# A hybrid decoder trunk: the 16x16 inverses on GpSimd, and an output projection cut at 12 of its 16 row tiles

## The chip, the cores and the metric

One core of a Trainium2 chip. The metric is the device time of one execution in microseconds (us), as a median of several. The matrix engine is TensorE (PE in the rows; PEld is its weight load), the vector engine VectorE (DVE), the scalar engine ScalarE (ACT), the general engine GpSimd (POOL); SyncE (SP) issues the weight loads from HBM.

## What is computed

Two decoder layers over 256 tokens of width 2048. Layer 0's mixer, the one that the change touches, has two halves behind one input projection: 8 HGRN2 heads (a gated linear recurrence) and 8 gated DeltaNet heads. Cut to what matters:

```
def gated_delta_chunked(q, k, v, beta, g):           # the "gdn" heads
    a_mat = einsum(kb, k) * decay * strict           # strictly lower triangular
    t_mat = triangular_solve(eye + a_mat, eye)       # the inverse of a unit triangle
    w, u  = t_mat @ (kb * exp(gam)), t_mat @ (v * beta)
    ...                                              # recurrence over chunks

def hgrn2_gdn_mixer(u, ...):
    proj = u @ w_in                                  # 2048 x 8208
    o_a = gated_head_norm(hgrn2_chunked(...))        # 8 heads, 1024 columns
    o_b = gated_head_norm(gated_delta_chunked(...))  # 8 heads, 1024 columns
    return concatenate([o_a, o_b]) @ w_out           # 2048 x 2048

def reference(x, ...):
    for layer in range(2):
        h = h + mixer(rmsnorm(h))                    # hgrn2 + gdn, then mamba2
        h = h + memory_cross_attention(rmsnorm(h))
        h = h + swiglu(rmsnorm(h))
    return rmsnorm(h)
```

All is float32.

## The kernel before

**Projections.** Every weight streams once from HBM in tiles of 128 partitions x 1024 numbers (two row tiles of 512 columns), named `wr`. `split` makes two reduced-precision parts of each: ScalarE casts it (`wh`), VectorE subtracts (`wl <- wr, wh`, both read from SBUF). Four buffers each of wr, wh and wl let this run a few tiles ahead. `xstat` then does six products for each row tile into two accumulators in PSUM (`acc`): these are called projection products below, and 12 of them use up one tile of wl. `project` calls `xstat` for four blocks of 512 output columns (`nb`), and VectorE adds each accumulator to the residual `h`; behind a block, a `done` function may turn it for the next layer's norm.

**The first mixer** (`hybrid`) runs `gdn(0)`, `gdn(1)`, `hgrn(0)`, `hgrn(1)`, each a group of four heads, and then the output projection, in two calls of `project`: row tiles 8 to 15 (the two gdn groups, `yb`), then 0 to 7 (the two hgrn groups, `ya`), the second with `done`. A group's small work (decays, masks, norms) is a chain over all engines. While a chain runs, TensorE does projection products of whatever is independent of it.

**The inverse in `gdn(g)`.** Four heads' triangular matrices `M` go to DRAM and come back as 64 diagonal blocks of 16x16, one to a partition (`U`). Starting from the identity in `x`, 15 steps of a multiplication into `w` and a subtraction from `x` invert them all; each needs the one before it. A copy turns the result over. The two go to DRAM (`scratch`, two stores) and return as `X` and `XT`, two DMAs each, all issued by GpSimd. Then three levels of products on TensorE (`mx <- XT, b` is each level's first) put together the whole inverse. `tt(pool, B, M, mb)` on GpSimd makes `b` (`b <- MD,big` in the rows).

**`hgrn(g)`** goes through seven levels; in each VectorE makes `tmp <- cv`, ScalarE takes the exponential, GpSimd multiplies the halves with k and q (`tmp <- tmp,kq`), and TensorE makes products. q comes over `tn` transposes and ScalarE's copy `kq <- tn`. The group ends in `finish`: products with `S` (`mx <- vt,D` or `uf,D`), `head_norm` (squares on ScalarE, sums and a reciprocal root in small steps on VectorE, scaled rows `b <- mx,hms,gate`, transposes `mx <- cst,b` on TensorE) and `head_out`.

**What sets the order.** The program is written in the order above; a list scheduler, working from modelled durations, then fixes for each engine the order in which its instructions stand. On the chip every engine takes its own in that order and waits at an instruction whose input isn't there. TensorE's place for a chain's next product is thus a count of projection products ahead of it. Names such as `b` stand for small scratch buffers of a pool.

Of the kernel before, what the change touches and what calls it, by code (L numbers as in the profile page):

```python
# [14 lines left out]
ALU = mybir.AluOpType  # L15
# [4 lines left out]
D = 2048  # L20
T = 256
KT = D // P
# [6 lines left out]
for _name, _w in (("norm_mix", 32), ("norm_xattn", 32), ("norm_mem", 32), ("norm_ffn", 32), ("norm_final", 16),  # L29
# [12 lines left out]

BLOCKS = {
    "hy_w_in": [(0, KT, n, 512) for n in range(0, 8192, 512)] + [(0, KT, 8080, P)],
    "hy_w_out": [(k, 8, n, 512) for k in (0, 8) for n in range(0, D, 512)],
    "ssd_w_in": ([(0, KT, n, 512) for n in range(0, 8192, 512)] + [(0, KT, n, 512) for n in range(8192, 10240, 512)]
                 + [(0, KT, 10176, P)]),
    "ssd_w_out": [(k, KT, n, 512) for k in (0, KT) for n in range(0, D, 512)],
# [9 lines left out]
FIRST = {}  # L58
# [20 lines left out]
def trunk(ctx: ExitStack, tc: tile.TileContext, A: dict, out: bass.AP):  # L79
    nc = tc.nc  # L80
    pe, act, dve, pool = nc.tensor, nc.scalar, nc.vector, nc.gpsimd
# [42 lines left out]
    def tt(e, o, a, b, op):  # L124
        e.tensor_tensor(o, a, b, op=op)  # L125
# [54 lines left out]
            mm(acc, wl, xh, False, k == KT - 1)  # L180
        return acc

    def xstat(W, n0, n, u, k0=0, nk=KT):

        accs = [pa.tile([P, n], F32, name="acc", tag="acc") for _ in range(2)]
        for k, wh, wl in wtiles(W, k0, nk, n0, n):
            for a in range(2):
                xh = u[k // 4][0][:, k % 4, a * P:(a + 1) * P]
                xl = u[k // 4][1][:, k % 4, a * P:(a + 1) * P]
                mm(accs[a], xh, wh, k == 0, False)  # L190
                mm(accs[a], xh, wl, False, False)
                mm(accs[a], xl, wh, False, k == nk - 1)
        return accs
# [125 lines left out]
    def blk(W, nb):  # L319
        return W[nb * 512:(nb + 1) * 512, :].rearrange("(k p) t -> p k t", p=P)  # L320

    def project(W, u, k0, nk, done=None, parts=None):
        for nb in range(4):
            n = 256 if nb == 3 and (W[0], k0, nb * 512, 512) not in FIRST else 512
            for c in range(0, 512, n):
                for a, acc in enumerate(xstat(W, nb * 512 + c, n, u, k0, nk)):
                    hb = h[nb][:, a, c:c + n]
                    tt(dve, hb, hb, acc, ALU.add)
                    if parts:
                        parts(nb, a, c, n)  # L330
            if done:
                done(nb)
# [130 lines left out]
    def hybrid(N, nxt):  # L463
# [47 lines left out]
        def gdn(g):  # L511
# [60 lines left out]
            for k in range(15):  # L572
                n, r = 15 - k, k + 1
                o, e = x[:, 0, 0:r, r:16], w[:, 0:r, r:16]
                tt(dve, e, x[:, 0, 0:r, k:r].to_broadcast([64, r, n]),
                   U[:, k:r, r:16].to_broadcast([64, r, n]), ALU.mult)
                tt(dve, o, o, e, ALU.subtract)
            dve.tensor_copy(x[:, 1].rearrange("p a b -> p b a"), x[:, 0])
            X = t4("X", [P, 2, 4, P])
            XT = t4("XT", [P, 2, 4, P])  # L580
            for q, (d, t) in enumerate(((d_x, X), (d_t, XT))):
# [135 lines left out]
        tt(dve, lb[:, 0], e2[:, 0], mx, ALU.mult)  # L717
        dve.tensor_scalar(lb[:, 1], lb[:, 0], -1.0, 1.0, op0=ALU.mult, op1=ALU.add)

        ya = [hgrn(0), hgrn(1)]  # L720
        Wo = ("hy_w_out", 0)
        project(Wo, yb, 8, 8)
        project(Wo, ya, 0, 8, lambda nb: nxt.block(nb, h[nb]))


    mem_r = []

    def xattn(layer, N, nxt):
# [43 lines left out]
        for i in range(2):  # L772
# [3 lines left out]
                for b in range(2):  # L776
                    mm(ps[:, x], v[:, b, m * P:(m + 1) * P], pT[b][:, m], x == 0 and b == 0, b == 1)
            split(hi[:, 2 * i:2 * i + 2], lo[:, 2 * i:2 * i + 2], ps)
        project(("xa_wo", layer), [(hi, lo)], 0, 4, lambda nb: nxt.block(nb, h[nb]))


    def ffn(layer, N, done=None, parts=None):
        b0 = 0
        for nblk in (4, 4, 3):
# [21 lines left out]
                late = sg  # L806
            turn(late)
            last = b0 + nblk == 11
            project(("ffn_w_down", layer), hid, 4 * b0, 4 * nblk, done if last else None, parts if last else None)
            b0 += nblk  # L810


    def ssd(N, nxt):
# [89 lines left out]
            ys.append(group(g, bct))  # L903
        r = ssa.column(2 * D)
        for nb in range(4):
            accs = xstat(Wo, nb * 512, 512, ys, KT)
            for a in range(2):
                p, hb = part[nb][:, a], h[nb][:, a]
                tt(dve, p, p, accs[a], ALU.add)
                stt(hb, p, r[:, a:a + 1], hb, ALU.mult, ALU.add)  # L910
            nxt.block(nb, h[nb])
# [115 lines left out]
```

## Time and profile before

| | |
|---|---|
| median of 3 runs | 2978.18 us (2977.99 to 2978.61) |
| the profiled execution | 2979.66 us, of which the span is 2977.9 us |
| first mixer (to the last transposes of its output) | 0 to about 595 us |
| TensorE | busy 2943.9 us, 99% of the span |
| VectorE, ScalarE, GpSimd | 58%, 51%, 9% |
| granted TensorE clock over the span | 0.996 |

The span runs from the first to the last instruction; the profiled execution's own time is 1.8 us above it. Times in rows count from the start of the span. Busy time of TensorE includes overlap of neighbouring products, so what it lacks to the span is only part of what it loses.

### The profile page before, as it was taken

How to read it: one execution, taken by the hardware profiler on the slowest of the kernel's cores; microseconds unless marked ns; L12 is line 12 of the kernel's file. 1: busy time of each engine (PE TensorE's matmuls, PEld its weight loads, DVE VectorE, ACT ScalarE, POOL GpSimd, SP SyncE). 2: the span in 40 equal slices, each digit the busy share in tenths (PEclk: the TensorE clock that was granted, in tenths of full speed). 3: DMA queues.
4: the chain of work that ended last, by engine and by line, in shares of the span. 5: the costliest groups of instructions: out<-in, count | busy, mean ns of one | idle time of the engine just before them, and what ended most of it. 6: DMA issues, size and time to landing. Idle time of an engine off the chain costs nothing.

```text
span 2977.9 us, 36564 instructions
## 1 busy us (share of the span) xinstructions
PE 2943.9 (99%) x13948; PEld 2443.6 (82%) x13948; DVE 1736.4 (58%) x2138; ACT 1517.2 (51%) x1939; POOL 258.8 (9%) x211
## 2 busy tenths in 40 slices
PE   9999999999999999999999999999999999999998
PEld 7888788788888888888888788878888888888887
DVE  6665568766455445455666646666665454455455
ACT  7545545565443443344567645766555444443444
POOL 1011203210000000000022300231000000000000
PEclk9999999999999999999999999999999999999999
DMA  7555444465666666666555556455666666666664
GB/s 282 171 166 156 158 137 131 136 198 169 190 187 195 191 191 187 195 190 185 180 160 157 159 187 187 153 156 164 190 198 186 190 190 192 191 190 191 194 188 148
DMA packets 152160, 533.35 MB, mean 179 GB/s; under 512 B 16592, under 2 KB 22864, under 8 KB 151984
## 3 DMA queue, kind: packets, MB, share of 16 engines
q1 hardware_dynamic: 150096, 526.15, 57.4%
q0 software_dynamic: 1472, 4.59, 0.6%
q8 instruction: 109, 1.79, 0.2%
q14 instruction: 67, 0.55, 0.1%
q10 hardware_dynamic: 416, 0.27, 0.0%
HBM read 526.49 MB, written 4.46 MB: 178 GB/s over the span
## 4 chain that ended last, share of the span: by engine, by line
PE 95%; DVE 1%; DMA 1%; ACT 1%; issue 1%; POOL 1%; SPq 0%; DVEq 0%; ACTq 0%; POOLq 0%
PE acc L122 87%; PE mx L122 5%; PE mx L280 1%; PE tn L280 1%; DMA wr<-in_memT 0%; POOL tmp L125 0%; PE mx L863 0%; DMA XT<-scratch 0%; DVE wl L125 0%; DMA scratch<-b 0%; ACT wh L157 0%; PE mx L438 0%; DVE tmp L125 0%; ACT u L254 0%; DMA wr<-in_hy_w_in 0%
## 5 line engine op out<-in xcount | busy, mean ns | idle before, releaser
L122 PE MATMUL acc<-wh,u 128*128 128x512 f32 (+1 forms) x7904 | 2457.9, 390 | 8.2 <-ACT wh L157 6.5
L125 DVE TENSOR_TENSOR wl<-wr,wh 128x1024 fp32r<-128x1024 f32 x980 | 1239.7, 1269 | 1076.4 <-ACT wh L157 1073.8
L122 PEld LDWEIGHTS acc<-wh,u 128*128 128x128 f32 x7904 | 1476.0, 188 | 307.2 <-ACT wh L157 6.5
L157 ACT CAST wh<-wr 128x1024 fp32r<-128x1024 f32 x980 | 1028.3, 1052 | 1144.6 <-PE acc L122 1070.1
L122 PE MATMUL acc<-wl,u 128*128 128x512 f32 (+1 forms) x3952 | 1539.2, 390 | 1.2 <-DVE wl L125 1.1
L122 PEld LDWEIGHTS acc<-wl,u 128*128 128x128 f32 x3952 | 744.4, 188 | 151.6 <-DVE wl L125 2.8
L125 POOL TENSOR_TENSOR tmp<-gh,cst 128x512 fp32r<-128x512 f32 x36 | 50.7, 1408 | 1297.6 <-ACT gh L157 845.0
L128 DVE SCALAR_TENSOR_TENSOR cv<-tn,cols,cv 128x255 f32<-128x255 f32 (+2 forms) x120 | 57.7, 481 | 31.1 <-ACT cv L353 28.5
L125 POOL TENSOR_TENSOR tmp<-tmp,kq 128x512 f32<-128x512 f32 x32 | 56.5, 1790 | 132.9 <-ACT tmp L670 129.1
L125 DVE TENSOR_TENSOR h<-h,acc 128x512 f32<-128x512 f32 (+1 forms) x84 | 52.2, 655 | 9.7 <-PE acc L122 9.5
L361 ACT ACTIVATE raw<-acc,r 128x512 f32<-128x512 f32 x66 | 43.3, 682 | 12.5 <-PE acc L122 10.6
L128 DVE SCALAR_TENSOR_TENSOR u<-mx,cols,u 128x256 fp32r<-128x256 f32 x96 | 43.2, 478 | 7.2 <-ACT u L301 4.3
L301 ACT ACTIVATE u<-mx,cols 128x256 fp32r<-128x256 f32 x80 | 35.0, 470 | 20.9 <-PE mx L280 16.0
L280 PE MATMUL tn<-cst,raw 128*128 128x128 f32 x272 | 44.9, 273 | 0.0
L280 PEld LDWEIGHTS tn<-cst,raw 128*128 128x128 f32 x272 | 34.5, 141 | 9.4
L125 POOL TENSOR_TENSOR tmp<-gl,cst 128x512 fp32r<-128x512 f32 x36 | 40.2, 1119 | 0.1
L125 DVE TENSOR_TENSOR u<-mx,u 128x512 fp32r<-128x512 f32 x48 | 31.0, 684 | 13.3 <-ACT u L157 13.3
L122 PE MATMUL mx<-tmp,mr 128*128 128x512 f32 x108 | 35.9, 415 | 0.0
L125 POOL TENSOR_TENSOR MD<-MD,b 128x1536 f32<-128x1536 f32 x8 | 34.9, 4361 | 1.2 <-ACT MD L412 1.2
L157 ACT CAST u<-mx 128x512 fp32r<-128x512 f32 x48 | 26.0, 592 | 17.2 <-PE mx L280 10.6
L308 ACT ACTIVATE b<-h 128x512 f32<-128x512 f32 x48 | 29.9, 624 | 2.2 <-DVE h L128 2.0
L122 PEld LDWEIGHTS mx<-tmp 128*128 128x128 f32 x240 | 28.2, 192 | 1.2 <-POOL tmp L125 0.5
(265 smaller groups left out, 1297.2 us busy)
## 6 DMA issues: line engine op xcount, KB each, us to landing
wr<-in_ffn_w_gate SPq DMA_DIRECT2D x176, 512.0 KB, 3.6
wr<-in_ffn_w_up SPq DMA_DIRECT2D x176, 512.0 KB, 3.6
wr<-in_ffn_w_down SPq DMA_DIRECT2D x176, 512.0 KB, 3.6
wr<-in_ssd_w_in SPq DMA_DIRECT2D x162, 512.0 KB, 3.7
wr<-in_hy_w_in SPq DMA_DIRECT2D x130, 512.0 KB, 3.7
wr<-in_ssd_w_out SPq DMA_DIRECT2D x64, 512.0 KB, 3.7
wr<-in_hy_w_out SPq DMA_DIRECT2D x32, 512.0 KB, 3.7
wr<-in_xa_wq SPq DMA_DIRECT2D x16, 512.0 KB, 3.6
```

The costliest lines, as they stand in the source:

```text
L122: pe.matmul(o, lhsT=lhsT, rhs=rhs, start=start, stop=stop, skip_group_check=True)
L125: e.tensor_tensor(o, a, b, op=op)
L128: dve.scalar_tensor_tensor(o, a, s, b, op0=op0, op1=op1)
L157: act.copy(hi, src)
L280: pe.transpose(ps[:, x, a * P:(a + 1) * P], src[a][:, c * P:(c + 1) * P], ident)
L301: act.activation(hi[:, c], ps[:, x], AF.Copy, scale=g)
L308: act.activation(t4("b2", [P, 512]), src[:, a], AF.Square, accum_out=self.ss[:, a, nb:nb + 1])
L361: act.activation(o[a], accs[a], func, scale=r[:, a:a + 1])
```

## The change

Three edits. (1) The 30 dependent multiplications and subtractions of the inverse, and the copy behind them, go from VectorE to GpSimd, in both gdn groups. (2) The output projection's first call takes 12 row tiles, those of both gdn groups and of the first hgrn group, into one accumulation; the second takes the 4 of the second hgrn group. The weights are stored in the new order of blocks. (3) `xstat` and `project` take lists of row ranges; the other callers do as before. The scheduler orders the new program anew.

```
 BLOCKS = {
-    "hy_w_out": [(k, 8, n, 512) for k in (0, 8) for n in range(0, D, 512)],
+    "hy_w_out": [(k, nk, n, 512) for k, nk in ((8, 8), (0, 4), (4, 4)) for n in range(0, D, 512)],
...
-    def xstat(W, n0, n, u, k0=0, nk=KT):
+    def xstat(W, n0, n, u, *rows):
 
         accs = [pa.tile([P, n], F32, name="acc", tag="acc") for _ in range(2)]
-        for k, wh, wl in wtiles(W, k0, nk, n0, n):
+        rows = rows or ((0, KT),)
+        nk = sum(r[1] for r in rows)
+        tiles = (t[1:] for r in rows for t in wtiles(W, *r, n0, n))
+        for k, (wh, wl) in enumerate(tiles):
...
             for k in range(15):
                 n, r = 15 - k, k + 1
                 o, e = x[:, 0, 0:r, r:16], w[:, 0:r, r:16]
-                tt(dve, e, x[:, 0, 0:r, k:r].to_broadcast([64, r, n]),
+                tt(pool, e, x[:, 0, 0:r, k:r].to_broadcast([64, r, n]),
                    U[:, k:r, r:16].to_broadcast([64, r, n]), ALU.mult)
-                tt(dve, o, o, e, ALU.subtract)
-            dve.tensor_copy(x[:, 1].rearrange("p a b -> p b a"), x[:, 0])
+                tt(pool, o, o, e, ALU.subtract)
+            pool.tensor_copy(x[:, 1].rearrange("p a b -> p b a"), x[:, 0])
...
         ya = [hgrn(0), hgrn(1)]
-        project(Wo, yb, 8, 8)
-        project(Wo, ya, 0, 8, lambda nb: nxt.block(nb, h[nb]))
+        project(Wo, yb + ya[:1], ((8, 8), (0, 4)))
+        project(Wo, ya[1:], ((4, 4),), lambda nb: nxt.block(nb, h[nb]))
```

How instructions stand on three places. First GpSimd in group 1, before: from the loads of M's blocks (`b_2121`) to the stores and gathers, with the first products of `hgrn(0)` (`tmp <- tmp,kq`) between.

```order
L571 MEMSET b_2123 64x16
L125 TENSOR_TENSOR b_2166<-MD,big 128x512
L125 TENSOR_TENSOR tmp<-tmp,kq 128x512
L125 TENSOR_TENSOR tmp<-tmp,kq 128x256x2
L125 TENSOR_TENSOR tmp<-tmp,kq 128x512
L125 TENSOR_TENSOR tmp<-tmp,kq 128x256x2
L582 DMA scratch_109<-b_2123 64x16x16
L582 DMA scratch_110<-b_2123 64x16x16
L584 DMA X<-scratch_109 128x4x128 x2
L584 DMA XT<-scratch_110 128x4x128 x2
```

And in the changed kernel, from the 20th of the 30 steps of the same inverse (`x` is `b_2123`, `w` is `b_2124`) onward:

```order
L125 TENSOR_TENSOR b_2123<-b_2123,b_2124 64x11x5
L125 TENSOR_TENSOR b_2124<-b_2123,b_2121 64x12x4
L125 TENSOR_TENSOR b_2123<-b_2123,b_2124 64x12x4
L125 TENSOR_TENSOR b_2124<-b_2123,b_2121 64x13x3
L125 TENSOR_TENSOR b_2123<-b_2123,b_2124 64x13x3
L125 TENSOR_TENSOR tmp<-tmp,kq 128x512
L125 TENSOR_TENSOR tmp<-tmp,kq 128x256x2
L125 TENSOR_TENSOR b_2124<-b_2123,b_2121 64x14x2
L125 TENSOR_TENSOR b_2123<-b_2123,b_2124 64x14x2
L125 TENSOR_TENSOR b_2124<-b_2123,b_2121 64x15
L125 TENSOR_TENSOR b_2123<-b_2123,b_2124 64x15
L581 COPY b_2123<-b_2123 64x16x16
```

The inverse now stands in GpSimd's queue, and the four `tmp` products stand within it: one behind the 20th step, one behind the 21st, two behind the 26th. Ahead of them `b_2166 <- MD,big` stands behind the first step. In group 0 the 30 steps stand alone, but for that one `b`; there XT's gather, which stood behind two `tmp <- gh` and `tmp <- gl`, now stands ahead of them.

Second TensorE at group 1's first product with XT, before (`acc_3220` and `acc_3221` are the accumulators of the second hgrn group's first projection):

```order
L122 MATMUL acc_3221<-wl_3243,u_94 128x512
L122 MATMUL acc_3221<-wh_3242,u_95 128x512
L122 MATMUL acc_3220<-wh_3260,u_159 128x512
L122 MATMUL acc_3220<-wl_3261,u_159 128x512
L122 MATMUL mx_2168<-XT_2159,b2_2166 128x128 x4
L122 MATMUL acc_3220<-wh_3260,u_160 128x512
L122 MATMUL acc_3221<-wh_3260,u_159 128x512
```

And in the changed kernel (`acc_3006` and `acc_3007` are those of the projection ahead of it):

```order
L122 MATMUL acc_3007<-wl_3101,u_207 128x512
L122 MATMUL acc_3007<-wh_3100,u_208 128x512
L122 MATMUL acc_3006<-wh_3118,u_255 128x512
L122 MATMUL acc_3006<-wl_3119,u_255 128x512
L122 MATMUL mx_2168<-XT_2159,b2_2166 128x128 x4
L122 MATMUL acc_3006<-wh_3118,u_256 128x512
L122 MATMUL acc_3007<-wh_3118,u_255 128x512
```

The product stands behind 1226 projection products before and behind 1178 now. The last product that group 1's M needs (`mx <- kq`) stood behind 1045 and stands behind 1019, so that 159 projection products and three sets of four `tn` transposes are now between the two, where there were 181 and the same three sets. In group 0 the M products stand where they stood (the last behind 515), and the first product with XT stands behind 655, where it was 680.

Third TensorE at the end of the second hgrn group, before: the last products with D, then the transposes of its normed output.

```order
L122 MATMUL acc_4470<-wh_4491,u_3208 128x512
L122 MATMUL acc_4470<-wl_4492,u_3208 128x512
L122 MATMUL acc_4470<-wh_4491,u_3209 128x512
L122 MATMUL mx_4002<-vt_3852,D_3714 128x128 x8
L438 MATMUL mx_4015<-cst_83,b2_4037 128x128 x2
L438 MATMUL mx_4016<-cst_83,b2_4037 128x128 x2
L438 MATMUL mx_4015<-cst_83,b2_4046 128x128 x2
L438 MATMUL mx_4016<-cst_83,b2_4046 128x128 x2
```

And in the changed kernel, from the same products with D:

```order
L122 MATMUL acc_4289<-wl_4330,u_2353 128x512
L122 MATMUL acc_4289<-wh_4329,u_2354 128x512
L122 MATMUL mx_4001<-vt_3852,D_3714 128x128 x4
L122 MATMUL mx_4002<-vt_3852,D_3714 128x128 x8
L122 MATMUL acc_4290<-wh_4329,u_2353 128x512
L122 MATMUL acc_4290<-wl_4330,u_2353 128x512
L122 MATMUL acc_4290<-wh_4329,u_2354 128x512
L122 MATMUL acc_4289<-wh_4347,u_2353 128x512
```

Behind the rows shown 49 projection products in all (of the 12-tile call) now come before the first of these transposes, where none stood. In the first hgrn group, 62 projection products stand between its last product with D and its transposes, where there were 84. Of the 384 products of the output projection, 288 now belong to the first call and 96 to the second.

## Rows read from the trace of the kernel before

**Rows 1.** The page of the whole execution: the span, then for each engine its busy time, its share of the span and its instructions.

```profile
span 2977.9 us, 36564 instructions
PE 2943.9 (99%) x13948; PEld 2443.6 (82%) x13948; DVE 1736.4 (58%) x2138; ACT 1517.2 (51%) x1939; POOL 258.8 (9%) x211
```

**Rows 2.** Waits of TensorE over the whole span, longest in total first: who waited for whom, us in total, times, longest.

```profile
PE mx L438 <- DVE b L128: 5.9, 2, 4.1
PE mx L122 <- DMA XT<-scratch: 5.4, 1, 5.4
PE acc L122 <- DVE wl L125: 1.1, 1, 1.1
```

**Rows 3.** Busy time of each engine in four stretches of 20 us (start:end, length, then busy time and instructions of PE, PEld, DVE, ACT and POOL), and behind them the granted TensorE clock as a share of 2.4 GHz, the DMA share and GB/s.

```profile
320.00:340.00 20.00, 14.17 (x61) 11.34 (x61) 14.06 (x26) 7.56 (x8) 5.98 (x7) 1.00 0.79 246
340.00:360.00 20.00, 19.38 (x101) 17.09 (x102) 5.74 (x7) 4.33 (x5) 2.58 (x2) 0.83 0.37 125
480.00:500.00 20.00, 18.20 (x83) 14.82 (x82) 19.93 (x32) 10.88 (x15) 8.08 (x4) 0.91 0.49 138
540.00:560.00 20.00, 15.65 (x76) 12.81 (x75) 9.72 (x28) 6.11 (x10) 0.00 (x0) 0.83 0.23 76
```

**Rows 4.** TensorE in order of time: start us, us, what; in brackets the idle time before it and who ended it. The first row is a piece of the chain of work that ended last, in the first FFN; the others are of the timeline: group 0's first product with XT, the last product that group 1's M needs, group 1's first product with XT, and the transposes that end the second hgrn group.

```profile
877.92 147.39 PE acc L122 x650
174.56 0.72 PE L122 MATMUL mx<-XT,b 128*128 128x128 f32 x5
290.66 0.59 PE L122 MATMUL mx<-kq 128*128 128x256 f32 x2
340.62 2.05 PE L122 MATMUL mx<-XT,b 128*128 128x128 f32 x8 [5.38 <-DMA XT<-scratch]
549.89 2.29 PE L438 MATMUL mx<-cst,b 128*128 128x128 f32 x8 [4.10 <-DVE b L128]
```

**Rows 5.** VectorE's timeline, the inverse's first row and its closing copy, in group 0 and in group 1 (64 partitions, so many elements in each).

```profile
143.57 0.79 DVE L125 TENSOR_TENSOR b<-b,b 64x15 f32<-64x15 f32 x4 [1.85 <-DMA b<-scratch]
159.45 0.38 DVE L578 COPY b<-b 64x256 f32<-64x256 f32 x1
299.44 0.37 DVE L125 TENSOR_TENSOR b<-b,b 64x15 f32<-64x15 f32 x2 [3.30 <-DMA b<-scratch]
326.72 0.38 DVE L578 COPY b<-b 64x256 f32<-64x256 f32 x1
```

**Rows 6.** GpSimd's timeline behind the inverse: the two DMAs that gather XT, as GpSimd issues them, in group 0 and in group 1.

```profile
168.94 1.53 POOL L584 DMA_DIRECT2D XT<-scratch  x2
334.19 1.49 POOL L584 DMA_DIRECT2D XT<-scratch  x2 [0.70 <-DMA scratch<-b]
```

**Rows 7.** GpSimd's instructions over the whole span, grouped with the shapes kept apart: line, engine, operation, out<-in, shape, count | busy us, mean ns of one | idle before.

```profile
L125 POOL TENSOR_TENSOR b<-b 128x256 f32<-128x256 f32 x22 | 16.5, 754 | 97.0 <-ACT b L221 97.0
L125 POOL TENSOR_TENSOR b<-MD,big 128x512 f32<-128x512 f32 x12 | 15.5, 1291 | 49.9 <-PE mx L122 49.7
L125 POOL TENSOR_TENSOR tmp<-tmp,kq 128x512 f32<-128x512 f32 x32 | 56.5, 1790 | 132.9 <-ACT tmp L670 129.1 <-ACT tmp L673 1.6 <-ACT tmp L672 1.3
L570 POOL MEMSET b<- 64x512 f32 x2 | 1.1, 545 | 0.0
L571 POOL MEMSET b<- 64x16 f32 x2 | 0.2, 120 | 0.1
```

**Rows 8.** Timelines of VectorE and GpSimd where both read SBUF at once, at 54 us and at 317 us. cst, gh, wr, wh, b, cv and kq lie in SBUF; tn and mx lie in PSUM.

```profile
53.95 1.23 DVE L125 TENSOR_TENSOR wl<-wr,wh 128x1024 fp32r<-128x1024 f32 x1
54.14 1.94 POOL L125 TENSOR_TENSOR tmp<-gh,cst 128x512 fp32r<-128x512 f32 x1 [21.78 <-ACT gh L157]
55.10 1.01 DVE L125 TENSOR_TENSOR gl<-gT,gh 128x16 fp32r<-128x16 f32 x1
56.19 1.04 POOL L125 TENSOR_TENSOR tmp<-gl,cst 128x512 fp32r<-128x512 f32 x1
56.03 1.50 DVE L128 SCALAR_TENSOR_TENSOR kq<-tn,cols,kq 128x255 f32<-128x255 f32 x3
316.83 3.04 DVE L125 TENSOR_TENSOR b<-b,b 64x63 f32<-64x63 f32 x2
```

**Rows 9.** VectorE in the stretches that matter for the inverse. The first two rows count the instructions on the tile wl alone (stretch, length, busy us, count, clock, DMA); the other two are groups within 299.44 to 334.85 us.

```profile
143.57:168.88 25.31, 12.18 (x10) 1.00 0.70 207
299.44:334.85 35.41, 15.28 (x13) 1.00 0.55 166
L650 DVE TENSOR_TENSOR_SCAN cv<-big,tmp 128x128 f32<-128x128 f32 x4 | 1.5, 400 | 0.0
L125 DVE TENSOR_TENSOR tmp<-cv 128x512 f32<-128x512 f32 x4 | 2.6, 678 | 0.0
```

**Rows 10.** ScalarE's copy of q in group 1's stage, and VectorE at the ends of the two hgrn groups: the last sum of squares and the first of the rows that scale the output, for the second group (546 us) and for the first (470 us).

```profile
315.99 0.57 ACT L642 COPY kq<-tn 128x512 f32<-128x512 f32 x1
546.46 0.69 DVE L431 TENSOR_REDUCE hms<-b 128x4 f32<-128x512 f32 x1
549.39 2.16 DVE L128 SCALAR_TENSOR_TENSOR b<-mx,hms,gate 128x128 f32<-128x128 f32 x8
470.72 1.34 DVE L431 TENSOR_REDUCE hms<-b 128x4 f32<-128x512 f32 x2
492.47 2.15 DVE L128 SCALAR_TENSOR_TENSOR b<-mx,hms,uf 128x128 f32<-128x128 f32 x8
```

More of the change, by code (lines that the diff above doesn't have):

```diff
@@ L320, in blk, with project @@
         return W[nb * 512:(nb + 1) * 512, :].rearrange("(k p) t -> p k t", p=P)
-    def project(W, u, k0, nk, done=None, parts=None):
+    def project(W, u, rows, done=None, parts=None):
         for nb in range(4):
-            n = 256 if nb == 3 and (W[0], k0, nb * 512, 512) not in FIRST else 512
+            n = 256 if nb == 3 and (W[0], rows[0][0], nb * 512, 512) not in FIRST else 512
             for c in range(0, 512, n):
-                for a, acc in enumerate(xstat(W, nb * 512 + c, n, u, k0, nk)):
+                for a, acc in enumerate(xstat(W, nb * 512 + c, n, u, *rows)):
                     hb = h[nb][:, a, c:c + n]
@@ L718, in hybrid @@
         dve.tensor_scalar(lb[:, 1], lb[:, 0], -1.0, 1.0, op0=ALU.mult, op1=ALU.add)
+        Wo = ("hy_w_out", 0)
         ya = [hgrn(0), hgrn(1)]
-        Wo = ("hy_w_out", 0)
-        project(Wo, yb, 8, 8)
-        project(Wo, ya, 0, 8, lambda nb: nxt.block(nb, h[nb]))
+        project(Wo, yb + ya[:1], ((8, 8), (0, 4)))
+        project(Wo, ya[1:], ((4, 4),), lambda nb: nxt.block(nb, h[nb]))
     mem_r = []
@@ L778, in xattn @@
             split(hi[:, 2 * i:2 * i + 2], lo[:, 2 * i:2 * i + 2], ps)
-        project(("xa_wo", layer), [(hi, lo)], 0, 4, lambda nb: nxt.block(nb, h[nb]))
+        project(("xa_wo", layer), [(hi, lo)], ((0, 4),), lambda nb: nxt.block(nb, h[nb]))
     def ffn(layer, N, done=None, parts=None):
@@ L808, in ffn @@
             last = b0 + nblk == 11
-            project(("ffn_w_down", layer), hid, 4 * b0, 4 * nblk, done if last else None, parts if last else None)
+            project(("ffn_w_down", layer), hid, ((4 * b0, 4 * nblk),), done if last else None, parts if last else None)
             b0 += nblk
@@ L905, in ssd @@
         for nb in range(4):
-            accs = xstat(Wo, nb * 512, 512, ys, KT)
+            accs = xstat(Wo, nb * 512, 512, ys, (KT, KT))
             for a in range(2):
```

## The prediction

> **What bounds the kernel now.** The page comes first: TensorE is busy for 99% of the span [rows 1], so nothing matters but what makes it wait or slows its clock. One projection product takes 147.39 / 650 = 0.2268 us where nothing disturbs it [rows 4], and their number doesn't change. The waits of TensorE come second: its two costliest single waits are in the first mixer [rows 2], and both lie at places that the change touches. One is group 1's first product with XT, for which TensorE idles 5.4 us on the gather; the other is the end of the second hgrn group, 4.1 us on VectorE's scaled rows [rows 4]. The windows come third, for what such a wait costs behind it: the granted clock, elsewhere 1.00, has a mean of 0.83 in the 20 us that follow or hold each of the two, and 0.91 at 480 us [rows 3]. [...]
>
> **The inverse before.** In group 0 it runs on VectorE from 143.57 to 159.83 us, in group 1 from 299.44 to 327.10, 27.7 us [rows 5]. Group 1's XT can be used at 340.62, which is 13.5 us behind the copy's end; its gather was issued at 334.19, as soon as the store had landed [rows 6]. In group 0 TensorE came to its product at 174.56 and didn't wait [rows 4].
>
> **When it must be done now.** TensorE's place is fixed by the order. Group 0: the product stands 25 projection products earlier, so TensorE is there at 174.56 - 25 x 0.2268 = 168.9. The start stays at 143.57, since the products for M stand where they stood. The gather of XT, at 168.94 before [rows 6], now stands directly behind X's, so I take group 1's 13.5 us for it. The chain on GpSimd has 168.9 - 143.6 - 13.5 = **11.8 us**; what it takes beyond that TensorE waits.
> Group 1: from the last M product (290.66) to TensorE's arrival at XT (340.62 - 5.38 = 335.24) were 44.6 us [rows 4]. Less a wait of 1.1 us for wl in between [rows 2], and less 22 x 0.2268 = 5.0 us for the products that now stand elsewhere, it is 38.5 us. The inverse started 299.44 - 290.66 = 8.8 us behind that M product. So the limit is 38.5 - 8.8 - 13.5 = **16.2 us**, against 27.7 before. (With before's numbers, 8.8 + 27.7 + 13.5 - 44.6 gives its wait of 5.4.)
>
> **What it takes on GpSimd.** No row shows such a step there. The nearest are 754 ns for 256 elements and 1291 ns for 512 [rows 7], which make 0.217 us fixed and 2.1 ns for an element. The 30 steps hold 1360 elements (15 to 64 each): 6.5 + 2.9 = 9.4 us. Bounds: 30 x 0.12 = 3.6 us by the MEMSET of 16, 30 x 0.754 = 22.6 us by the 256-element row [rows 7]. I take 9.4, since the line through two shapes of the same operation is nearer than a MEMSET. The copy of 256 is 0.55 us by the MEMSET of 512 [rows 7], and the `b <- MD,big` that stands behind the first step 1.29. Group 0: 11.2 us of work. Group 1 has four tmp products inside, 1.29 each if nothing is in the way (5.2): 16.4 us.
>
> But GpSimd isn't alone. The rows at 54 us show it: wl began at 53.95 and held VectorE until 55.18; GpSimd's tmp<-gh, begun at 54.14, took 1.94 us, the same shape behind it 1.04. Then VectorE's gl, 16 elements, took 1.01 us beside it. At 317 us two 63-element steps of the inverse took 3.04 us together [rows 8]. The three kq<-tn at 56.03, one input from PSUM, kept to 0.5 us each [rows 8]. So a VectorE instruction with two SBUF inputs and a GpSimd one take turns, whole. [...]
> What this does to 30 short dependent steps is the choice of this forecast. GpSimd's tmp products, mean 1.79 us against 1.29 [rows 7], are lengthened by 1.39; at that price the two chains take 15.6 and 22.8 us. But there an instruction of GpSimd is as long as one of wl, and VectorE waits about as often. A step of 0.3 us holds VectorE up hardly at all, while each wl holds the chain for 1.2 us, and the chain always has a step ready. So I take what VectorE leaves free. Group 0: wl holds 12.18 of 25.31 us [rows 9], 0.52 is left, 11.2 / 0.52 = 21.6 us, a **wait of 9.8 us**. Group 1: wl, the scans and tmp<-cv hold 15.28 + 1.5 + 2.6 = 19.4 of 35.41 us [rows 9], 0.45 is left. TensorE arrives 38.5 - 8.8 = 29.7 us into the chain, with 13.4 us of it done; then wl dries up, and the other 3.0 us go on beside about two more wl (2.4): 35.1 us, a **wait of 18.9 us** in place of 5.4.
>
> **The output projection.** At the end of the second hgrn group 49 products, 11.1 us, now stand between the D products and the transposes. From the last sum of squares to the scaled rows VectorE took 546.46 to 549.39 [rows 10], and two wl that now stand between add 2.4: covered. Gone are 20 - 15.65 = 4.35 us of idle TensorE and the 3.4 us of clock [rows 3]: **7.8 us**. In the first hgrn group the cover shrinks by 22 products, 5.0 us, but VectorE, which took from 470.72 to 492.47 there [rows 10], loses work of about that size from between (residual additions and wl). I take nothing for it; what could be late is again those transposes, by up to 3 us. The 96 products at the end, over four blocks, must cover the same turning of h as 192 did; the next layer's queries take the blocks in order, so I count nothing.
>
> **Sum.** Group 0: +9.8, and +3.4 for the clock behind it. Group 1: +18.9 - 5.4 = +13.5, the clock lost as before. VectorE without the inverse no longer holds up wl: -1.1. Projection: -7.8. Together +17.8 on the profiled execution's 2979.66 (its span of 2977.9 [rows 1] and 1.8 around it), which is 1.5 above the median of the runs: 2978.2 + 17.8 = **2996 us**, slower by 0.6%.
>
> **Rivals.**
> *The turns cost nothing: faster.* At 11.2 us group 0's chain makes its 11.8. Group 1's can't be shorter than its queue lets it: the last tmp products wait for ScalarE's copy of q, 16.5 us into the chain before [rows 10, 5] and some 2.3 us (10 products) earlier now; with two products, four steps and the copy it ends at about 19, a wait of 2.8. Sum: -2.6 - 1.1 - 7.8 = -11.5, **2967 us**. For it: the steps take 5.7 us on VectorE's own rows, and the queue of VectorE is rid of them and of 1.85 and 3.30 us of waiting for U [rows 5]. Against it: rows 8. It decides if the chains aren't lengthened by more than about 1.2.
> *They cost about what the projection gives: no change.* Lengthened by 1.39, 15.6 and 22.8 us: waits of 3.8 (+3.4 of clock) and 6.6 (+1.2), less 8.9: -0.5, **2978 us**.
> *A step costs what 256 elements cost.* Work of 24.5 and 29.6 us by the upper bound: TensorE arrives with 13.2 and 13.4 done, and waits about 27 and 32 us: 27.2 + 3.4 + 26.7 - 8.9 = +48, **3027 us**.
> *The projection's cut gives nothing* (another wait takes the place of the one that is filled, in the first hgrn group or in the four short blocks): +7.8 on the forecast, **3004 us**.
>
> **How the numbers follow.** Two executions agree within a few tenths of a us; 0.2%, 6 us, is what I count as a change. Chances: the forecast 0.50, steps as dear as the upper bound 0.08, the projection without gain 0.10, all slower; no change 0.10; faster 0.22. The likeliest case's own range, with steps 0.1 us cheaper or dearer and the hgrn end at its bounds, is 2986 to 3008. The range has to reach to the faster case and leaves out the dearest: 2965 to 3008. Faster 0.22, same 0.10, slower 0.68.
>
> **What would show it.** Group 0's inverse on GpSimd spans about 22 us with gaps or long steps wherever a wl runs, TensorE idles some 10 us on XT near 169 us, with a clock under 1.00 behind it; group 1's spans about 35 us and its wait for XT is three times what it was. The wait on VectorE's b at the second hgrn group is gone. I am wrong if the steps stand close together beside wl, at 0.3 us each: then the wait at 169 us is missing, and the sum is that of the first rival.

## The result, and the profile after

The changed kernel takes **2983.26 us**, median of 22 runs (2978.55 to 2988.01), and the kernel before, run beside it, 2978.48 (2976.59 to 2981.61): ratio 1.0014, 95% interval 1.0007 to 1.0020. So it is slower by 4.8 us, where 17.8 were forecast: the sign is right, the size is not, and 0.14% lies below what the prediction counts as a change. The profiled execution took 2980.13 us, only 0.5 more than the one before. Of e5 below one execution, 3689.18 us at a granted clock of 0.751, is no part of its ratio.

The page answers [rows 1]: the span, busy time and instructions.

```profile
span 2978.3 us, 36559 instructions
PE 2941.1 (99%) x13948; PEld 2442.4 (82%) x13948; DVE 1727.9 (58%) x2076; ACT 1515.6 (51%) x1938; POOL 296.7 (10%) x273
```

62 instructions went from VectorE to GpSimd. TensorE's waits answer [rows 2] (us in total, times, longest):

```profile
PE mx L122 <- DMA XT<-scratch: 13.7, 2, 10.8
PE acc L122 <- ACT wh L157: 6.5, 1, 6.5
PE mx L122 <- POOL tmp L125: 1.6, 3, 1.0
PE acc L122 <- DVE gate L128: 0.8, 1, 0.8
```

XT is waited for twice, 13.7 us in place of 5.4. The wait for `b` at the ends of the hgrn groups is gone at both. The 6.5 us for the first wh at the start of the span are the same before and are TensorE's longest single wait there; [rows 2] leaves them out. The stretches of [rows 3] and those around 170 and 430 us (columns as there):

```profile
160.00:180.00 20.00, 17.02 (x83) 14.32 (x82) 11.29 (x15) 9.67 (x12) 9.66 (x10) 0.91 0.62 194
320.00:340.00 20.00, 9.24 (x40) 7.64 (x39) 5.39 (x4) 3.75 (x4) 13.25 (x16) 0.77 0.64 207
340.00:360.00 20.00, 20.00 (x112) 17.39 (x111) 7.47 (x9) 7.59 (x9) 3.25 (x3) 0.97 0.29 82
420.00:440.00 20.00, 19.02 (x114) 17.21 (x114) 15.92 (x16) 7.99 (x8) 7.94 (x4) 0.92 0.44 129
480.00:500.00 20.00, 20.00 (x119) 17.39 (x118) 19.48 (x31) 11.60 (x16) 10.65 (x5) 1.00 0.50 158
540.00:560.00 20.00, 20.00 (x94) 16.57 (x93) 14.67 (x31) 8.86 (x11) 0.00 (x0) 1.00 0.58 165
```

Before, the two that [rows 3] doesn't have were:

```profile
160.00:180.00 20.00, 20.00 (x97) 16.69 (x96) 15.03 (x19) 11.88 (x16) 9.93 (x10) 1.00 0.80 239
420.00:440.00 20.00, 18.43 (x104) 15.72 (x103) 12.95 (x16) 13.96 (x15) 4.57 (x4) 1.00 0.32 97
```

At 480 and 540 us TensorE is now busy throughout at full clock; at 160 and 320 us it has lost time and clock; at 420 us it is busy for longer, but at a clock of 0.92 in place of 1.00. TensorE's two products with XT, against [rows 4]:

```profile
171.02 2.04 PE L122 MATMUL mx<-XT,b 128*128 128x128 f32 x8 [2.98 <-DMA XT<-scratch]
...
337.26 2.04 PE L122 MATMUL mx<-XT,b 128*128 128x128 f32 x8 [10.76 <-DMA XT<-scratch]
```

TensorE came to them at 168.0 and 326.5 us (start less wait), within 1 us of what the prediction made of its places (168.9; 288.4 + 38.5). GpSimd's timeline in group 0 and, behind "...", in group 1, against [rows 5, 6]:

```profile
142.63 0.30 POOL L125 TENSOR_TENSOR b<-b,b 64x15 f32<-64x15 f32 x1 [1.55 <-DMA b<-scratch]
142.89 1.29 POOL L125 TENSOR_TENSOR b<-MD,big 128x512 f32<-128x512 f32 x1
144.14 14.70 POOL L125 TENSOR_TENSOR b<-b,b 64x15 f32<-64x15 f32 x29
158.90 0.63 POOL L581 COPY b<-b 64x256 f32<-64x256 f32 x1
...
297.60 0.20 POOL L125 TENSOR_TENSOR b<-b,b 64x15 f32<-64x15 f32 x1 [2.46 <-DMA b<-scratch]
326.46 0.62 POOL L581 COPY b<-b 64x256 f32<-64x256 f32 x1
333.25 1.49 POOL L587 DMA_DIRECT2D XT<-scratch  x2 [0.17 <-issue]
```

Group 0's chain takes 142.63 to 159.53, 16.9 us (forecast 21.6); group 1's 297.60 to 327.08, 29.5 (forecast 35.1). From the copy's end to the product with XT are 11.5 and 10.2 us (forecast 13.5).

**A ledger.** For all kernels below one sum is used: from the start of each TensorE product to the start of the next, less the median of that distance for its shape, added up over a stretch. It holds idle time and low clock together. Its total plus 2930 us is each profiled time within 0.5 us, so no more than that is left out. The two rows of the changed kernel differ by up to 2.0 us in one stretch, and a profiled execution lies up to 3.7 us from its kernel's median (e7), so small differences between two rows say little. In us, of one profiled execution each:

```
stretch (us)                  0-140 140-200 200-300 300-360 360-420 420-460 460-500 500-600 600-700 700-end total
what ends there                     XT, g 0         XT, g 1         levels  hgrn 0  hgrn 1
before                          5.9     0.5     3.0    10.2     0.5     2.2     4.4     8.2     6.6     8.8  50.1
changed                         4.8     5.0     3.1    13.1     0.5     5.5     1.0     1.0     7.1     8.7  49.9
changed, once more (e12)        5.1     7.0     3.1    13.9     0.5     4.1     1.0     1.0     7.2     8.8  51.5
inverses alone (e1)             5.1     5.2     3.1    13.2     0.5     5.6     1.0     2.5     6.4     8.8  51.3
cut alone (e2)                  5.8     0.5     3.0    10.6     0.5     2.2     9.5     5.5     9.7     8.8  55.9
group 0 on GpSimd, cut (e3)     5.1     2.4     3.1     9.4     0.5     4.1     8.6     1.2     7.0     8.8  50.3
changed, XT later (e5)          4.8     0.5     3.1     2.7     0.5     2.9     8.2     7.0     6.7     8.7  45.1
three calls (e6)                5.0     0.5     3.0    10.3     0.5     2.2     3.4     2.8     7.7     8.7  43.9
three calls, XT later (e7)      5.6     0.5     3.0     7.3     0.5     3.0     4.5     8.6     9.8     8.8  51.5
before, XT later (e8)           5.1     0.5     3.0     5.6     0.5     2.9     3.1    12.5     6.9     8.7  48.7
three calls, GpSimd (e10)       6.3     5.4     3.1    13.5     0.5     4.0     1.0     1.9     7.2     8.8  51.6
half inverse (e11)              6.3     0.5     3.0     7.4     0.4     2.2     4.1     1.8     7.2     8.7  41.6
e10, group 0 later (e13)        5.3     1.2     3.1    11.2     0.5     7.1     7.1     1.7     7.7     8.8  53.7
```

The change lost 4.5 us at group 0's XT, 2.9 at group 1's, 3.4 at the levels of the first hgrn group, and won 3.4 and 7.2 at the two hgrn ends. At the levels TensorE's waits add up to about as much as before (1.8 and 1.6 us); the rest is clock, 0.92 and 0.91 in the two stretches of 20 us from 420 us on, where it was 1.00.

### The profile page after: what moved, and what is told of

It reads as the page before. It is cut to its first block, busy times and chain, and to the rows that moved or that the text cites. A ratio compares the mean times of both kernels' runs of the same rounds, so it can differ in the third digit from the quotient of the medians.

```text
span 2978.3 us, 36559 instructions
## 1 busy us (share of the span) xinstructions
PE 2941.1 (99%) x13948; PEld 2442.4 (82%) x13948; DVE 1727.9 (58%) x2076; ACT 1515.6 (51%) x1938; POOL 296.7 (10%) x273
## 4 chain that ended last, share of the span: by engine, by line
PE 92%; issue 3%; POOL 3%; DMA 2%; ACT 1%; DVE 0%; SPq 0%; DVEq 0%; POOLq 0%; ACTq 0%
PE acc L122 84%; PE mx L122 5%; POOL b L125 1%; PE mx L283 1%; POOL tmp L125 1%; PE tn L283 1%; DMA wr<-in_memT 0%; DMA XT<-scratch 0%; DMA scratch<-b 0%; PE mx L866 0%; DMA scratch<-MD 0%; DMA b<-scratch 0%; ACT wh L157 0%; ACT u L257 0%; DMA wr<-in_hy_w_in 0%
## 5 line engine op out<-in xcount | busy, mean ns | idle before, releaser
L125 POOL TENSOR_TENSOR b<-b,b 64x15 f32<-64x15 f32 (+7 forms) x60 | 32.5, 542 | 8.2 <-DMA b<-scratch 4.0
```

## Experiments

Ratios are against the kernel before, run on the same chip beside each set (its medians: 2979.04 for e1, e2, e3 and e5; 2977.71 for e6, e7, e8; 2979.54 for e10, e11; 2978.77 for e13). The time with XT is called group 0's or group 1's.

### The two halves of the change apart

The inverses alone (the blocks of the weights, not shown, as before too):

```
-        project(Wo, yb + ya[:1], ((8, 8), (0, 4)))
-        project(Wo, ya[1:], ((4, 4),), lambda nb: nxt.block(nb, h[nb]))
+        project(Wo, yb, ((8, 8),))
+        project(Wo, ya, ((0, 8),), lambda nb: nxt.block(nb, h[nb]))
```

> The inverses on GpSimd as in the change, the output projection in two calls of 8 row tiles as before. TensorE's places: XT of group 0 behind 655 projection products and of group 1 behind 1178, as in the changed kernel; the end of the second hgrn group now has 41 projection products before its transposes without the cut (0 before the change, 49 with it). Theory A (the cut itself gives little once the inverses have moved the order, since the order fills that end anyway): the waits for XT are 3 and 11 us as in the changed kernel, no wait at the second hgrn end, time within 3 us of the changed kernel's 2983. Theory B (the cut is worth the 7.8 us that the prediction gave it): the wait at 540 to 560 us is back, and the time is 2990.

Measured 2982.64, ratio 1.0012 (1.0002 to 1.0021). Theory A: the second hgrn end lost only 2.5 us in 500 to 600, without the cut.

The cut alone (`tt(dve, ...)` and `dve.tensor_copy` in the inverse, the rest as changed):

> The output projection cut at 12 row tiles as in the change, the inverses on VectorE as before. TensorE's places of XT are before's (680 and 1045+181). Theory A (the cut gives the 7.8 us and nothing is late for it; the loss is all in the inverses): group 1's wait for XT stays at 5 us, the wait at the second hgrn end is gone, 2971 us. Theory B (the cover taken from the first hgrn group, 56 products where 84 stood, makes its transposes late): a wait of some 5 us at about 490 us, and 2976 to 2978 us.

Measured 2983.59, ratio 1.0015 (1.0007 to 1.0024): worse than either theory. Its two costliest waits at the mixer's chains:

```profile
PE mx L122 <- DMA XT<-scratch: 5.6, 1, 5.6
PE mx L441 <- DVE b L128: 3.2, 1, 3.2
```

and two stretches:

```profile
480.00:500.00 20.00, 16.07 (x65) 12.60 (x65) 16.66 (x27) 9.56 (x13) 6.75 (x4) 0.83 0.32 109
540.00:560.00 20.00, 20.00 (x114) 17.43 (x113) 13.20 (x29) 7.13 (x9) 0.00 (x0) 1.00 0.39 122
```

The wait at 540 us is gone as forecast, but the one at 480 us, 1.8 before, is 3.2 at a clock of 0.83. In the ledger +5.0 there and +3.2 at 600 to 700 (2.1 of it a wait for GpSimd's `ss`, which before doesn't have) stand against -2.7. What gdn's rows could cover before now waits for the first hgrn group, because both are one accumulation; in e6 below, where they are apart, the loss at 480 us is not there.

Group 1's inverse back on VectorE, the rest as changed (`ie = pool if g == 0 else dve`):

> As changed, but group 1's inverse stays on VectorE; group 0's is on GpSimd. TensorE comes to group 0's XT behind 655 products, to group 1's behind 1202 (1178 in the changed kernel, 1226 before). Theory A (the loss of the change is made in group 1, where four tmp products stand inside the chain): group 0's wait is 3 us with 1.5 us of clock, group 1's 5 us or less, 2976 us. Theory B (the loss is made in group 0, by the clock behind its wait): group 0 as in the changed kernel and 2983 us.

Measured 2982.16, ratio 1.0014 (1.0005 to 1.0023). Neither theory: the waits for XT fell to 1.7 and 5.0 us as A has it, and the 6.3 us so won (ledger, 140 to 360) were lost again at the first hgrn end, +7.6, where 48 projection products stand instead of 62. These 14 products are 3.2 us of it. VectorE's scaled rows also came 3.0 us later, 17.5 us behind the last products with D where it was 14.5: four of its steps of 0.17 us took 1.35 to 1.47 us beside GpSimd's products `tmp <- tmp,kq`, in the changed kernel one did.

### Is the wait only the chain's end less TensorE's place?

As changed, with the first products with XT placed later:

```
+                    if s == 16 and a == 0:
+                        tc.cur_priority += (560, 900)[g]
                     for m in range(4):
                         mm(ps[:, m], B[:, m], XT[:, a, m])
+                    if s == 16 and a == 0:
+                        tc.cur_priority -= (560, 900)[g]
```

> As changed in all its instructions, but the first products with XT are given to the scheduler as later in the program, so that TensorE comes to them behind 674 (group 0) and 1242 (group 1) projection products instead of 655 and 1178; the second has 195 since the last product that M needs, where it had 159. Theory A (the loss is the chain's end less TensorE's place, and nothing else): in group 0 the wait of 3 us is gone, in group 1 36 x 0.227 = 8.2 us of the 11 are gone; 2983 - 3 - 1.5 - 8 = 2970 us. Theory B (what costs is the turns at SBUF: wl is late and TensorE waits for it elsewhere, or what the products with XT feed comes late further on): the waits for XT shrink as said, others grow, and the time stays at 2980 or more.

Measured 2976.22, ratio 0.9994 (0.9985 to 1.0003). Both theories are half right. TensorE in order of time, at group 1's XT and at the end of the first hgrn group:

```profile
338.60 0.46 PE L122 MATMUL mx<-XT,b 128*128 128x128 f32 x2 [0.43 <-DMA XT<-scratch]
...
472.33 0.50 PE L122 MATMUL acc<-wh,u 128*128 128x512 f32 x1 [2.46 <-DVE raw L128]
...
481.10 0.50 PE L122 MATMUL acc<-wl,u 128*128 128x512 f32 x1 [1.67 <-DVE wl L125]
...
488.41 0.59 PE L441 MATMUL mx<-cst,b 128*128 128x128 f32 x2 [2.01 <-DVE b L128]
```

The losses at XT are gone (14.9 us of the ledger), and 13.2 us appear between 460 and 600 us, less 2.6 that 420 to 460 won. By the medians 7 us of the 13 forecast stay.

The kernel before with only that edit, `(0, 900)[g]`:

> The kernel before, and group 1's first products with XT given to the scheduler as later (1242 projection products ahead instead of 1226); 85 products at the first hgrn end (84 before), none at the second, as before. Theory A: the wait for XT 5.4 to 1.8 us, the 3 us of clock behind it gone, the second hgrn end as before: 2979 - 6.6 = 2972 us. Theory B (what is saved there is waited for further on): 2977 us or more.

Measured 2980.47, ratio 1.0008 (0.9999 to 1.0017): theory B. In the ledger 4.6 us are won at XT and 4.3 lost at 500 to 600; the profile nets 1.4 less than before's, the median is 2.8 more.

### More products to stand between, and a shorter chain

Three calls instead of two or of the cut, the inverses on VectorE:

```
+        project(Wo, yb, ((8, 8),))
+        project(Wo, ya[:1], ((0, 4),))
+        project(Wo, ya[1:], ((4, 4),), lambda nb: nxt.block(nb, h[nb]))
```

> The inverses on VectorE as before, the output projection in three calls: 8 row tiles of the gdn groups, 4 of the first hgrn group, 4 of the second. TensorE's order is before's up to the end of the first hgrn group (84 projection products in front of its transposes, where the cut at 12 tiles alone left 56); at the end of the second, 39 products (8.8 us) now stand where none stood. Theory A (the cut's price is the cover that it takes from the first hgrn group, because the gdn rows can't be projected before that group is done): nothing is lost at 480 us, the 7 us at the second end are gained, 2972 us. Theory B (four more blocks to add on VectorE, or 96 products at the end that don't cover the turning of h, take it back): 2977 us or more, with waits at 560 to 660 us that before doesn't have.

Measured **2974.11**, ratio 0.9988 (0.9980 to 0.9997): faster than both kernels. Theory A in kind, half of it in size:

```profile
480.00:500.00 20.00, 18.17 (x87) 14.38 (x87) 19.83 (x32) 10.94 (x14) 8.08 (x4) 1.00 0.47 151
540.00:560.00 20.00, 18.90 (x99) 15.64 (x98) 15.94 (x36) 8.06 (x11) 0.00 (x0) 1.00 0.42 133
```

At 480 us TensorE is busy 18.17 us as before (18.20 in [rows 3]), at 540 18.90 instead of 15.65, both at full clock. XT's stretch is unchanged (10.3).

The same with group 1's XT later:

> As the three calls with the inverses on VectorE, and group 1's first products with XT given to the scheduler as later: 1242 projection products ahead instead of 1226, 197 since the last product that M needs (181 before). The first hgrn end keeps 85 products, the second has 9. Theory A (a wait is the chain's end less TensorE's place, at each chain apart): group 1's wait falls from 5.4 to 1.8 us and the 3 us of clock behind it go; the second hgrn end waits 2 us with little clock; 2979 - 3.6 - 3 - 3 = 2970 us. Theory B (products are a fixed stock and the sum of the waits stays): as much as the three calls alone.

Measured 2977.48, ratio 1.0001 (0.9992 to 1.0009): nearer to theory B, and 3.4 us above the three calls alone, where B had the same. Against e6, 3.0 us are won at XT and 5.8 lost again at the second hgrn end, where 9 products stand instead of 39 (in an execution 3.7 us above the median).

The three calls with the inverses on GpSimd:

> The inverses on GpSimd as in the change and the output projection in three calls (8, 4 and 4 row tiles) in place of the cut at 12. TensorE's places as in the changed kernel (XT behind 655 and 1178 products, 62 products at the first hgrn end), 53 at the second. Beside the three calls with the inverses on VectorE it tells what the inverses' move is worth where both have the same supply of projection products. Theory A (the move costs a wait at each XT that the earlier places give back later; the two chains are about as long as before): within 3 us of the three calls' 2974. Theory B (the waits of 3 and 11 us at XT are lost in full): 2974 + 3 + 1.5 + 5.5 = 2984 us.

Measured 2982.32, ratio 1.0011 (1.0003 to 1.0020): theory B. At XT 8.2 us more were lost than in e6 (140 to 360), and 3.2 won back at the two hgrn ends.

The last with group 0's XT later, `(560, 450)[g]`:

> The inverses on GpSimd and the three calls, and group 0's first product with XT given to the scheduler as later: behind 674 projection products instead of 655; group 1's behind 1205, and still 158 behind the last product that M needs (159). The first hgrn end has 83 products (62), the second 56 (53). Theory A (a wait is the chain's end less TensorE's place): group 0's wait of 3.3 us goes with the clock behind it, group 1's 10.5 us stay, 2982.3 - 3.3 - 1.7 = 2977 us. Theory B (what is saved there is waited for further on): 2981 us or more.

Measured 2983.85, ratio 1.0018 (1.0009 to 1.0027): theory B. TensorE in order of time:

```profile
173.45 0.46 PE L122 MATMUL mx<-XT,b 128*128 128x128 f32 x2 [0.55 <-DMA XT<-scratch]
...
435.20 0.79 PE L122 MATMUL acc<-wh,u 128*128 128x512 f32 x1 [4.06 <-DVE gate L128]
...
495.56 0.72 PE L122 MATMUL acc<-wl,u 128*128 128x512 f32 x1 [3.17 <-DVE wl L125]
```

Group 0's wait is 0.6 us, and 9.2 us more were lost at 420 to 500. These waits are for projections themselves: an accumulator isn't emptied or a tile isn't split, because VectorE's queue (at 435 us ScalarE's too) holds the next chain's work ahead of that; before the second wait four of VectorE's small steps took 1.43 to 1.55 us each beside GpSimd's products. The first hgrn group's transposes, behind 83 products, have no wait now; the projections among these have.

Before, with half of group 1's inverse left out:

```
-            for k in range(15):
+            for k in range(7 if g == 1 else 15):
```

> The kernel before, with steps 8 to 15 of group 1's inverse left out (half of the computation of that inverse is missing from the result). Its chain is some 13 us shorter; TensorE comes to group 1's XT 24 projection products (5.4 us) earlier, and 32 products now stand at the end of the second hgrn group, where none stood; the projection isn't cut. Theory A (products between the chains are one supply, and a us less of chain in gdn pays wherever TensorE waits next): no wait for XT and none at the second hgrn end: 2979 - 5.4 - 3.1 - 7.3 = 2963 us. Theory B (only the wait at XT itself is affected): 2970 us.

Measured 2974.65, ratio 0.9985 (0.9976 to 0.9994). Less of the chain went than the 13 us expected: the steps left out had taken 5.8 us (320.9 to 326.7 before), and the copy grew by 3.2. VectorE's timeline, the inverse's first steps and its copy, then GpSimd's beside the copy:

```profile
299.89 0.37 DVE L125 TENSOR_TENSOR b<-b,b 64x15 f32<-64x15 f32 x2 [3.36 <-DMA b<-scratch]
...
318.73 3.61 DVE L578 COPY b<-b 64x256 f32<-64x256 f32 x1
```

```profile
319.06 3.03 POOL L125 TENSOR_TENSOR tmp<-tmp,kq 128x512 f32<-128x512 f32 x2
```

and TensorE's:

```profile
334.02 2.05 PE L122 MATMUL mx<-XT,b 128*128 128x128 f32 x8 [4.58 <-DMA XT<-scratch]
```

The chain is 22.5 us instead of 27.7, and XT came 6.6 us earlier (334.02 against 340.62). With TensorE there 5.8 us earlier (329.4 against 335.2) the wait at XT hardly fell. Still 4.9 us were gained; in the ledger most of it is at the second hgrn end (8.2 to 1.8), and 2.8 at XT and the clock behind it. That is theory A's kind, at the size of what was really cut.

### The turns between VectorE and GpSimd

```
+            if name == "hy_w_in":
+                act.copy(wh, raw)
+                dve.tensor_scalar(wl, raw, 0.0, None, op0=ALU.mult)
```

> As changed, but for the input projection of the first mixer VectorE makes wl as 0 times wr, an instruction with one input from SBUF, where it subtracted wh from wr (two); the low parts of these weights are thus left out of the result. Measured is the inverse of group 0 on GpSimd, alone in its queue but for one product b. Theory A (a two-input instruction of VectorE and one of GpSimd keep each other out): no step is stretched to 1.1 us or more, and the chain takes 16.9 - 5 x 0.9 = 12.4 us instead of 16.9. Theory B (GpSimd waits for any instruction of VectorE on SBUF): some five steps are still stretched, and the chain takes 15 to 17 us.

One execution, 2971.14 us. First the changed kernel, one step beside one wl, in VectorE's and in GpSimd's timeline:

```profile
147.58 1.23 DVE L125 TENSOR_TENSOR wl<-wr,wh 128x1024 fp32r<-128x1024 f32 x1 [1.12 <-ACT wh L157]
```

```profile
147.68 1.29 POOL L125 TENSOR_TENSOR b<-b,b 64x55 f32<-64x55 f32 x1
```

and steps of group 0's chain grouped by shape (count, busy us, mean ns, idle before):

```profile
L125 POOL TENSOR_TENSOR b<-b,b 64x39 f32<-64x39 f32 x4 | 2.8, 694 | 0.3
L125 POOL TENSOR_TENSOR b<-b,b 64x64 f32<-64x64 f32 x2 | 1.5, 743 | 0.2
L125 POOL TENSOR_TENSOR b<-b,b 64x63 f32<-64x63 f32 x4 | 1.3, 313 | 0.3
L125 POOL TENSOR_TENSOR b<-b,b 64x48 f32<-64x48 f32 x4 | 1.1, 273 | 0.3
```

Undisturbed steps (the x63 and x48) take 0.27 to 0.31 us, with 0.08 from one to the next. The step that met a wl ended 0.16 us behind it, after 1.29 us. Five of the 30 were so stretched, to 1.11 to 1.29 us (two of the four x39, one of the two x64): 16.9 less 5 x 0.9 is 12.4 us, against 11.2 of work in the forecast. Now wl with one input, on VectorE:

```profile
143.44 0.69 DVE L171 TENSOR_SCALAR wl<-wr 128x1024 fp32r<-128x1024 f32 x1 [2.48 <-PE acc L122]
```

and the chain on GpSimd, its timeline and two of the groups:

```profile
140.39 0.63 POOL L125 TENSOR_TENSOR b<-b,b 64x15 f32<-64x15 f32 x1 [3.09 <-DMA b<-scratch]
...
142.23 11.81 POOL L125 TENSOR_TENSOR b<-b,b 64x15 f32<-64x15 f32 x29
154.11 0.63 POOL L585 COPY b<-b 64x256 f32<-64x256 f32 x1
```

```profile
L125 POOL TENSOR_TENSOR b<-b,b 64x39 f32<-64x39 f32 x4 | 2.0, 496 | 0.3
L125 POOL TENSOR_TENSOR b<-b,b 64x64 f32<-64x64 f32 x2 | 0.6, 308 | 0.2
```

It takes 14.35 us (140.39 to 154.74). Five steps are still stretched, but by 0.3 to 0.5 us each. So each theory is half right: no step reaches A's 1.1 us, but the chain isn't down to 12.4; five steps are stretched as B has it, but the chain is under its 15 to 17 us. What counted here is how long a wl held VectorE, 0.69 us in place of 1.23 for the same 1024 elements, whether with one input or two: five steps were stretched beside the one as beside the other. Why a wl with one input takes little over half the time no run shows.

### The changed kernel again

> The changed kernel unaltered, for a second profiled execution, since the first (2980.1) lies 3 us under the median of its runs. Theory A (what differs between its executions is whether TensorE's clock falls behind the long wait for XT): a time of 2983 or more goes with a granted clock under 0.9 in the 20 us behind 337 us, where the first profile shows 0.5 us lost. Theory B (it is the arrival of weights, that is waits for wr, wh or wl anywhere): the clock behind XT is as in the first profile, and the waits for the splits are longer.

One execution, 2981.75 us, 1.6 above the first:

```profile
160.00:180.00 20.00, 16.45 (x67) 13.45 (x66) 9.66 (x14) 9.06 (x12) 9.99 (x10) 0.83 0.56 178
340.00:360.00 20.00, 20.00 (x107) 17.54 (x107) 6.16 (x7) 6.89 (x9) 3.82 (x3) 0.88 0.25 79
```

The clock behind both XT is lower (0.91 to 0.83, 0.97 to 0.88), 2.0 and 0.8 us in the ledger; at 420 to 460 it won 1.5. The splits' waits are as they were. This is theory A's mechanism, though the execution is not one of 2983. The span's granted clock has a mean of 0.9945 over the 22 runs of the changed kernel and of 0.9968 over the 96 of before beside the experiments. 0.0023 x 2980 = 6.9 us is an upper estimate of what that costs, as part of the low clock lies in idle time: in the first profile TensorE was idle for 6.4 of the 10.2 us for which the granted clock was 0.50 at group 1's XT (330.85 to 341.09). The medians are 4.8 us apart, the two profiled executions 0.5 and 2.1 above before's; the rest may be clock as well, but no profile of such an execution shows it.

## Why the prediction was right in sign and wrong in size

- **Places, starts, step price: right.** TensorE's two arrivals within 1 us; the steps 0.27 to 0.31 us where 0.25 to 0.35 were worked out; the chain's start 9.2 us behind the M product (8.8).
- **The turns: right in kind, the share failed.** "So I take what VectorE leaves free" gave wl (in group 1 with the scans and `tmp <- cv`) 0.48 and 0.55 of the time. A wl cost the chain its remaining 0.9 us, once, and only 5 met a step in group 0, 4.5 of 16.9 us or 0.27. In group 1 it was eleven steps of 1.13 to 1.29 us and four of 0.62, about 11 of 29.5 or 0.38. The share was taken from stretches that go on behind the inverse, where wl was lengthened or catching up (while the inverse itself ran, wl held 0.45 and 0.37), and it was let grow with the chain. It cost 4.7 and 5.6 us.
- **The tail: too long.** "I take group 1's 13.5 us for it": 11.5 and 10.2. In group 1 the gather took 4.0 us from issue to use (333.25 to 337.26), where it took 6.4 before ([rows 4, 6]).
- With these two the waits come out: 3.0 and 10.8 us instead of 9.8 and 18.9. The clock behind group 0's was 1.6 us in the first profile, where the granted clock was 0.50 for 3.4 us (170.42 to 173.84). The 3.4 us taken for it, and again in the 7.8 of the projection, are 20 x 0.17 by [rows 3]; before's trace has a granted clock of 0.50 for 6.8 us at each of the two waits (339.82 to 346.65, 548.04 to 554.86), and half of that is 3.4. Group 1's clock was taken "as before"; at 340 to 360 us it is 0.97 in place of 0.83, so that stretch lost only 2.9 us, though the wait grew by 5.4. The 1.1 us of waiting for wl are gone, as taken.
- **The second hgrn end: 7.2 us won (7.8 taken), but not by the cut.** e1 wins 5.7 of it without. Moving the inverses had already put that end's D products 63 projection products earlier (behind 1761, not 1824), which leaves products to stand behind them. And the cut by itself loses: e2 wins 2.7 us at this end and loses 5.0 at the first.
- **"I take nothing for it" at the first hgrn end:** 3.4 us were won there, and 3.4 not foreseen were lost at the levels around 430 us. That they cancel is luck. Five lines, VectorE and GpSimd before, then VectorE (two) and GpSimd in the changed kernel, show the first:

```profile
485.66 1.50 DVE L128 SCALAR_TENSOR_TENSOR hms<-sm,hms 128x8 f32<-128x8 f32 x1
483.11 8.08 POOL L125 TENSOR_TENSOR tmp<-tmp,kq 128x512 f32<-128x512 f32 x4 [21.10 <-ACT tmp L670]
...
481.45 1.51 DVE L128 SCALAR_TENSOR_TENSOR hms<-sm,hms 128x8 f32<-128x8 f32 x1
483.00 0.17 DVE L125 TENSOR_TENSOR sm<-hms 128x8 f32<-128x8 f32 x1
480.91 2.03 POOL L125 TENSOR_TENSOR tmp<-tmp,kq 128x512 f32<-128x512 f32 x1 [19.66 <-ACT tmp L673]
```

From the last sum of squares to the scaled rows VectorE now takes 12.8 us instead of 20.4 ([rows 10]: 472.06 to 492.47). Three wl and two additions to `h` are gone from between, as the prediction argued (about 5 us), and one small step is stretched beside GpSimd's products where three were (2.6 us less). So 62 products, 5.0 us less of cover, are enough, where 84 left a wait of 1.8 us.

With the right sizes the prediction's sum is +3.0 + 1.6 + 5.4 - 1.1 - 7.8 = +1.1, and the profiles differ by +0.5. That is in part luck as well: the clock that group 1 didn't lose is not in it, and the last term came true by the other edit. Also, executions of one kernel don't "agree within a few tenths": the 22 before spread over 5.0 us, the 22 changed over 9.5. Of its rivals the one with steps lengthened by 1.39, 2978 us, came nearest; its chain for group 0 was near too (15.6 us; 16.9 measured), its chain for group 1 was not (22.8; 29.5).

The larger fault is in the form of the sum: it priced two edits apart that aren't independent. By calls and place of the inverses, the ratios are

```
output projection      inverses on VectorE   on GpSimd
two calls, 8 + 8       1 (before)            1.0012 (e1)
cut, 12 + 4            1.0015 (e2)           1.0014 (the change)
three, 8 + 4 + 4       0.9988 (e6)           1.0011 (e10)
```

The inverses' move costs 3.6, nothing, or 6.8 us, and the cut 4.5 us or nothing. Each ratio is known to about 0.0009, 2.7 us, so of the three prices of the move only 6.8 us and nothing stand clearly apart. The reading that fits most of the runs is that one supply of products stands between the chains of this mixer: a later or earlier place moves a wait (e3, e7, e8, e13), and what pays is a shorter chain (e11) or more products that may stand there (e6). It is not shown to be exact. e5 gained 7 us by places alone, and the order on VectorE and GpSimd changes with each edit, so that the chains themselves get longer or shorter (e3, and the first hgrn end above).

## To carry to other kernels

Where a scheduler places the matrix engine's products anew, price a wait as the chain's end less the engine's place, but then ask from which other chain the products between were taken; only the sum over the stage counts. Let independent row tiles keep a call of their own: an accumulation is as late as its latest operand (e2 lost 5.0 us at the first hgrn end, e6 nothing). The chain of short steps beside another engine's long instructions paid here per instruction met (its remaining time, five times 0.9 us in group 0), not the other's busy share; and the other engine's own short steps paid in the same way (VectorE's of 0.17 us took 1.46 to 1.51 us beside GpSimd's products).

## What was not expected of the hardware

A copy of 256 elements on VectorE, 0.38 us in [rows 5], took 3.61 us in e11 and ended 0.25 us behind GpSimd's two products (322.34; 319.06 + 3.03): this one-input instruction of VectorE waited as well. Its steps of 0.17 us at the first hgrn end took 1.46 to 1.50 us beside four such products before, three of the eleven. And an identical program lost the clock behind the same wait to different depths, 0.91 and 0.83 in two executions.
